# A gated hybrid layer on one core: second mixer's decay exponentials two steps sooner, the last pairs of probabilities times values at adjacent steps, output projection in 512-column products

## The chip, the cores and the metric

The kernel runs on one core of one Trainium2 chip. The metric is the device time of one execution in microseconds. A core has five engines that run side by side, each through its own instructions in order: TensorE (PE in the profile, with PEld for its weight loads), VectorE (DVE), ScalarE (ACT), GpSimd (POOL), and SyncE (SP), which here issues DMAs. They wait for each other by semaphores. The profiler records one execution; the median is over runs without the profiler's page.

## The reference, cut to what matters

One layer over 256 tokens of width 1024. A token-wise modulation (shift, scale and gate computed from a vector `c`) and an RMS norm give `h`. One wide projection of `h` yields thirteen pieces, which feed two mixers; their outputs are gated, added, projected once more and added to `x`.

```python
h = _rmsnorm(x, norm_w) * (1 + scale) + shift
(qa, ka, va, za, qm, km, vm, zm, om, ig, fg, ga, gm) = jnp.split(h @ w_in, SPLIT_IDX, axis=-1)
...
ya = merge(_moba_attention(qa, ka, heads(va, ATT_HEADS), rel_bias))
ya = (ya * jax.nn.silu(za)) @ w_att_proj
...
qk = jax.nn.silu(_causal_dwconv(jnp.concatenate([qm, km], axis=-1), conv_w, conv_b))
hm = _mlstm_chunkwise(q, k, v, ig + b_igate, fg + b_fgate)
...
ym = (merge(hm).astype(x.dtype) * jax.nn.silu(zm)) @ w_ml_proj
y = jax.nn.sigmoid(ga) * ya + jax.nn.sigmoid(gm) * ym
return x + gate * (y @ w_out)
```

The first mixer is causal attention of 8 heads of 128 over the 256 tokens, with a bias by distance. The second is a linear attention of 4 heads of 256, in which a score of a query t and a key s is multiplied by a decay exp(e_s - m_t), where e and the running maximum m come from cumulative sums of the log forget gates and the input gates.

## The kernel before, in words

**Products.** Every large product is done in three: both operands are split into a high part (rounded by a cast) and a low part (the rest), and high x high, high x low and low x high are added in PSUM. The weights come from HBM as f32 into `raw` buffers of 1 MB; ScalarE casts a piece to `wh` (line 448), and VectorE (for a few steps GpSimd) subtracts to get `wl` (line 452).

**Steps.** After a first phase (normalisation, modulation, and the projections for the attention's queries and keys) the rest is a list of chunks of 512 output columns, four steps each; a step takes two blocks of 128 rows of the contraction. In the order of the list, with the steps of each: va 0 to 11, za 12 to 19, qm 20 to 27, km 28 to 35, the attention's projection att 36 to 43, then zm, vm, om, ga, gm, the second mixer's projection ml, and out. A chunk is of one of two kinds. In "ws" chunks (za, qm, km, att, ga, gm, ml) the weights are stationary and the 256 tokens stream: 24 products of 256 columns a step (lines 1006 to 1009). In "tok" chunks the tokens are stationary and 512 weight columns stream: 12 products a step (lines 999 to 1001; 344 columns wide for va). The chunks of out have code of their own: the first half in lines 987 to 994, the second in lines 1011 to 1022.

**Order.** The program's order is written out by hand. In step g the main loop (a) splits the weights of step g + 4, with the functions of `hooks_between` put between cast and subtraction, (b) at a chunk's first step evicts the chunk before and takes an accumulator, (c) calls the step's functions in `hooks`, in the order in which `at(step, fn)` registered them, (d) issues the weight loads that have become possible (`pump`), and (e) issues the step's products. Each engine runs what falls to it in that order. `at(s, f)` puts f into step s.

**Buffers.** Accumulators of chunks ("mm") rotate through two PSUM buffers, so chunk n + 2 can start only when chunk n has been read out. Smaller products ("aux") rotate through four. There are five `wh` and five `wl` buffers.

**What the change and the steps of the prediction touch.**

- `conv` (lines 676 and 682) reads a chunk of qm or km out of PSUM: for each quarter of two blocks ScalarE does the last tap with the bias (two instructions), then VectorE the three others (six). qm's first half is read in steps 24 and 25, and the SiLU of each (line 687) follows a step later.
- The second mixer's decay is prepared by `gates_0` to `gates_7`, `gates_T` and `gates_D`. `gates_5` (step 17) writes -m to a DRAM buffer `md`, and to GE an exponential (line 565). `gates_6` reads `md` back, spread over all partitions, into `NM`. `gates_7` copies and masks NM on GpSimd. `gates_T` transposes GE on TensorE (line 587) and VectorE copies the result to `gc` (line 589). `gates_D` is eight exponentials of ScalarE on NM with gc as bias (lines 595 and 596). NM is used from the chunk zm on.
- `att_PT` transposes one head's probabilities on TensorE and copies them. `att_av` (lines 642 to 650) takes a pair of heads: four products of values and probabilities on TensorE, the multiplication by `za` on VectorE (yf), a cast on ScalarE (yah), and the low part on GpSimd (yal). yah and yal are what the att chunks stream.
- `ev_out` (lines 859 to 862) evicts a piece of the output on VectorE, adds x and stores it.

Of the kernel before, what the change touches and what calls it, by code (L numbers as in the profile page):

```python
# [17 lines left out]
KT = 8  # L18
# [48 lines left out]
def tile_hybrid(ctx: ExitStack, tc: tile.TileContext, x, c, params2, w_row, w_va, ada_mod, ada_gate,  # L67
                w_in, w_att_proj, w_ml_proj, w_out, out):
    nc = tc.nc
# [94 lines left out]
    def modulate(k, parts="ij"):  # L164
        kc = slice(k, k + 1)
        src = xnT[:, k] if k else xps[0][:, 0]
        if "i" in parts:
            nc.scalar.activation(hTh[:, k], src, AF.Identity, scale=Ab[:, kc], bias=Bb[:, kc])
        if "j" not in parts:
            return  # L170
        hf[k] = ph.tile([128, S], F32, name="hf", bufs=2)
        if k:
            nc.scalar.activation(hf[k], src, AF.Identity, scale=Ab[:, kc], bias=Bb[:, kc])
        else:
            nc.vector.tensor_scalar(hf[k], src, Ab[:, kc], Bb[:, kc], op0=OP.mult, op1=OP.add)
# [4 lines left out]
    def split_hi(k, c0, c1, copy=nc.scalar.copy):  # L180
        if k not in wsp:
            wsp[k] = (ph.tile([128, NR], F32R, name="wrh", bufs=3), ph.tile([128, NR], F32R, name="wrl", bufs=3))
        copy(wsp[k][0][:, c0:c1], wrow[k][:, c0:c1])  # L183
# [49 lines left out]
    for j in range(4):  # L233
        n, q = divmod(j, 2)
        nc.tensor.matmul(pc[:, n, q * 256:(q + 1) * 256], pick[:, j:j + 1].to_broadcast([128, 128]), cparts,
                         start=q == 0, stop=q == 1, skip_group_check=True)
# [41 lines left out]
    def some(*what):  # L278
        return lambda k: [mm_row(k, ch, (i,)) for ch, i in what]
# [23 lines left out]
    for step in P1_STEPS:  # L303
        op, k = step[0], int(step[1])
        if op == "L":
            next_loads(k)
        else:
            dict(C=modulation, H=modulate, R=rel_prep, K=keep_clock, T=x_transposes, t=x_copy, B=open_banks,
                 D=lambda k: x_transposes(k, (0,)), E=lambda k: x_transposes(k, (1,)),
                 w=lambda k: split_hi(k, 0, 512), x=lambda k: split_hi(k, 512, 1024), y=lambda k: split_hi(k, 1024, NR),  # L310
# [4 lines left out]
                 a=modulation_scale, b=modulation_shift, i=lambda k: modulate(k, "i"), j=lambda k: modulate(k, "j"),  # L315
                 P=lambda k: mm_row(k, 0), Q=lambda k: mm_row(k, 1, (0, 1)), q=lambda k: mm_row(k, 1, (2,)),
                 N=lambda k: mm_row(k, 2), M=lambda k: mm_row(k, 3),
                 n=some((2, 0), (2, 1), (3, 0), (3, 1)), m=some((2, 2), (3, 2)),
# [30 lines left out]
    def done(name, half):  # L349
        return 4 * (C[name, half] + 1)  # L350
# [83 lines left out]
    whl = {}  # L434
# [6 lines left out]
    def split(g, between=()):  # L441
        li, ks, cs = raw_of[g]
        w = rawt[li][:, ks, cs]
        n = chunks[g // 4]["n"]
        at0 = WS_AT if chunks[g // 4]["kind"] == "ws" else 0
        h = hl.tile([128, RING], F32R, name="wh", bufs=HB)[:, at0:at0 + 1024].rearrange("p (k n) -> p k n", k=2)[:, :, 0:n]
        l = hl.tile([128, RING], F32R, name="wl", bufs=HB)[:, at0:at0 + 1024].rearrange("p (k n) -> p k n", k=2)[:, :, 0:n]
        nc.scalar.copy(h, w)  # L448
        for fn, a in between:
            fn(*a)  # L450
        e = nc.gpsimd if g in pool_lo else nc.vector
        e.tensor_tensor(l, w, h.bitcast(F32), op=OP.subtract)  # L452
        whl[g] = (h, l)
# [3 lines left out]
    def at(step, fn, *a):  # L457
        hooks.setdefault(step, []).append((fn, a))
# [201 lines left out]
    def ev_za(pt, half):  # L660
        if half == 0:
            T["za"] = slot("s0", [128, AH, S], F32, "zat")
        nc.scalar.activation(T["za"][:, 4 * half:4 * half + 4], pt, AF.Silu)
# [191 lines left out]
    def ev_out(pt, c0, n, t):  # L855
        cs = slice(c0, c0 + n)
        o = hl.tile([128, n], F32, name="o", tag="scr", bufs=2)
        if c0 < 512:
            nc.vector.tensor_tensor(o, pt, T["gateb"][:, cs], op=OP.mult)
            pt = o  # L860
        nc.vector.tensor_tensor(o, pt, T["x"][:, t, cs], op=OP.add)
        nc.sync.dma_start(o2[:, t, cs], o)
# [23 lines left out]
    for h in range(AH):  # L886
# [1 line left out]
        between(A0 + h, att_qk, h)  # L888
        hooks_between.setdefault(A0 + 3 + h, []).insert(0, (att_PT, (h,)))
        at(A0 + h, att_exp, h)  # L890
    for step, fn in ((12, gates_3), (14, gates_copy), (15, gates_4), (17, gates_5), (19, gates_6), (20, gates_7),
                     (21, gates_T), (23, gates_D)):
        at(step, fn)
    for nm in ("qm", "km"):
        for hf in range(2):
# [3 lines left out]
                at(s + q + 1, conv_silu, hf, nm, q)  # L899
    for q in range(2):  # L900
        at(done("za", 0) + 2 + 2 * q, att_av, 2 * q)
        at(done("za", 1) + 2 + 2 * q, att_av, 4 + 2 * q)
    s = 4 * C["zm", 0]
    for half in range(2):
        at(s + 5 * half, ml_split, half)
# [26 lines left out]
    mmt = {}  # L932

    def pump():
        n = 0
        while n in consumed:
            n += 1
        issue(n + 6)
# [11 lines left out]
    for g in range(NG):  # L950
        ci, kp = divmod(g, 4)
        ch = chunks[ci]
        if g + A < NG:
            split(g + A, hooks_between.get(g, []))
            consumed.update(li for li in cons.get(g + A, []) if li not in gate_loads)
        if kp == 0:
            if ci > 0:
                pc = chunks[ci - 1]
                if pc["name"] in EV and ci - 1 != C["za", 0]:
                    EV[pc["name"]](mmt[ci - 1], pc["half"])  # L960
                elif pc["name"] == "out":
                    for t in range(2):
                        ev_out(mmt[ci - 1][:, t], pc["half"] * 512, 512, t)
            sh = [128, 2, 512] if ch["kind"] == "tok" else [128, 4, 256]
            if ci < NCH - 1:
                mmt[ci] = ps.tile(sh, F32, name="mm", bufs=2)
                if ch["kind"] == "tok":
                    mmt[ci] = mmt[ci][:, :, 0:ch["n"]]
        for fn, a in hooks.get(g, []):
            fn(*a)  # L970
        if g == A0 + AH - 1:
            ev_za(mmt[C["za", 0]], 0)
        if g in gate_left:
            consumed.add(gate_left[g])
        pump()
        if g == NG - 8:
            load_x()
        sh_, sl_ = (hTh, hTl) if ch["stat"] is None else (T[stat[ch["stat"]][0]], T[stat[ch["stat"]][1]])
        wh, wl = whl[g]
        if ci == NCH - 1:  # L980
            continue
        for kk in range(2):
            k = 2 * kp + kk
            first, last = k == 0, k == KT - 1
            if ch["name"] == "out":

                for i in (0, 1):
                    for t, c0 in ((0, 0), (0, 256), (1, 0), (1, 256)):
                        a = (sh_, sl_)[i][:, k, t * 128:(t + 1) * 128]
                        cs = slice(c0, c0 + 256)  # L990
                        for w in (wh, wl)[:2 - i]:
                            nc.tensor.matmul(mmt[ci][:, t, cs], a, w[:, kk, cs],  # L992
                                             start=first and i == 0 and c0 == 0 and w is wh,
                                             stop=last and i == 1 and c0 > 0, skip_group_check=True)
            elif ch["kind"] == "tok":
                for t in range(2):
                    a, b = sh_[:, k, t * 128:(t + 1) * 128], sl_[:, k, t * 128:(t + 1) * 128]
                    o = mmt[ci][:, t]
                    nc.tensor.matmul(o, a, wh[:, kk], start=first, stop=False)  # L999
                    nc.tensor.matmul(o, a, wl[:, kk], start=False, stop=False)  # L1000
                    nc.tensor.matmul(o, b, wh[:, kk], start=False, stop=last)  # L1001
            else:
                for i in range(4):
                    cs = slice(i * 128, (i + 1) * 128)
                    o = mmt[ci][:, i]
                    nc.tensor.matmul(o, wh[:, kk, cs], sh_[:, k], start=first and i % 2 == 0, stop=False,  # L1006
                                     skip_group_check=True)
                    nc.tensor.matmul(o, wh[:, kk, cs], sl_[:, k], start=False, stop=False, skip_group_check=True)  # L1008
                    nc.tensor.matmul(o, wl[:, kk, cs], sh_[:, k], start=False, stop=last and i % 2 == 1,  # L1009
                                     skip_group_check=True)  # L1010
    ci = NCH - 1
    for t, c0, n in ((0, 0, 512), (1, 0, 256), (1, 256, 256)):
        pt = ps.tile([128, n], F32, name="mm", bufs=2)
        for k in range(KT):
            a, b = T["yh"][:, k, t * 128:(t + 1) * 128], T["yl"][:, k, t * 128:(t + 1) * 128]
            for c1 in range(0, n, 256):
                wh, wl = (w[:, k % 2, c0 + c1:c0 + c1 + 256] for w in whl[4 * ci + k // 2])
                o = pt[:, c1:c1 + 256]
                nc.tensor.matmul(o, a, wh, start=k == 0 and c1 == 0, stop=False, skip_group_check=True)  # L1019
                nc.tensor.matmul(o, a, wl, start=False, stop=False, skip_group_check=True)  # L1020
                nc.tensor.matmul(o, b, wh, start=False, stop=k == KT - 1 and c1 + 256 == n, skip_group_check=True)  # L1021
        ev_out(pt, 512 + c0, n, t)


# [51 lines left out]
```

## Time and profile before

| | |
|---|---|
| median of 3 runs | 357.51 us (357.04 to 357.94) |
| the profiled execution | 357.09 us |
| its span | 355.2 us |
| its mean granted TensorE clock | 0.995 |
| HBM read, written | 76.14 MB, 1.25 MB |

How to read the profile: the page gives, for each engine, the time in which it was busy, its share of the span and its instructions; the chain that ended last (what released what, followed back from the last instruction); and groups of instructions. A timeline's row gives start and duration in us, the engine, the line of the kernel, the operation, the tile written and the tiles read, the shape, and the count of instructions merged in the row; in brackets stands the idle time before it and what ended it. A stretch's row gives its window, then for each of PE, PEld, DVE, ACT and POOL the busy time and the count, then the granted TensorE clock (1.00 is full), the DMA share and GB/s. Products on TensorE overlap in a pipeline: a row's duration is that of one product from start to end, and what a product costs in a row of them is the distance between starts.

### The profile page before, as it was taken

The page shows a single profiled execution, that of the slowest core. Times are in us where ns is not written, and L with a number is a line of the kernel's source. Part 1 is how long each engine was busy: PE and PEld are TensorE (multiplying, and loading weights), DVE is VectorE, ACT ScalarE, POOL GpSimd, SP SyncE. Part 2 cuts the span into 40 slices and gives each one's busy share as a digit, 9 for nine tenths or more (in the row PEclk, how much of TensorE's full clock was granted, in tenths as well). Part 3 has the DMA queues.
Part 4 walks back from the last instruction along what each step waited for, and adds up shares of the span by engine and source line. Part 5 has one row for each costly group of instructions (what it writes and reads, how often), then busy time and mean ns, then how long its engine had stood idle before and what let it go on. Part 6 is the DMA issues. An engine that isn't in the chain of part 4 may idle for free.

```text
span 355.2 us, 6174 instructions
## 1 busy us (share of the span) xinstructions
PE 346.5 (98%) x2432; PEld 325.6 (92%) x2432; DVE 245.9 (69%) x369; ACT 213.5 (60%) x331; POOL 90.8 (26%) x81
## 2 busy tenths in 40 slices
PE   6999999999999997999999999999999999999996
PEld 6887889999999997999998888888899999999996
DVE  6999987967975326768875593764465874569861
ACT  4868889799777376666636554545646364544410
POOL 5700004950205261554104252000011320451000
PEclk9999999999999999899999999999999999999999
DMA  8999999880741850394784837649219129191011
GB/s 304 414 416 415 415 419 405 247 316 14 275 189 60 258 218 0 127 387 137 279 317 128 346 118 238 237 158 382 53 45 375 54 99 369 68 294 62 2 61 59
DMA packets 23516, 77.79 MB, mean 219 GB/s; under 512 B 3000, under 2 KB 4928, under 8 KB 22848
## 3 DMA queue, kind: packets, MB, share of 16 engines
q1 hardware_dynamic: 23336, 76.87, 58.8%
q10 hardware_dynamic: 152, 0.53, 0.4%
q8 instruction: 19, 0.31, 0.3%
q14 instruction: 9, 0.07, 0.1%
HBM read 76.14 MB, written 1.25 MB: 218 GB/s over the span
## 4 chain that ended last, share of the span: by engine, by line
PE 93%; ACT 2%; DVE 2%; DMA 1%; issue 0%; POOL 0%; DVEq 0%; ACTq 0%; POOLq 0%
PE mm L1006 14%; PE mm L1008 14%; PE mm L1009 14%; PE pm L198 12%; PE mm L999 8%; PE mm L1000 8%; PE mm L1001 8%; PE mm L992 3%; DVE qmT L682 1%; PE xps L263 1%; DMA xt<-in_x_dram 1%; PE mm L1021 1%; PE mm L1020 1%; PE mm L1019 1%; PE aux L492 1%; PE aux L604 1%
## 5 line engine op out<-in xcount | busy, mean ns | idle before, releaser
L452 DVE TENSOR_TENSOR wl<-raw,wh 128x1024 fp32r<-128x1024 f32 (+1 forms) x92 | 117.6, 1289 | 65.7 <-ACT wh L448 65.7
L448 ACT CAST wh<-raw 128x1024 fp32r<-128x1024 f32 (+1 forms) x100 | 100.4, 1014 | 59.8 <-PE mm L1008 25.7
L1006 PE MATMUL mm<-hTh,wh 128*128 128x256 f32 x320 | 91.2, 285 | 2.3 <-DVE qmT L682 2.3
L1008 PE MATMUL mm<-hTl,wh 128*128 128x256 f32 x320 | 89.7, 280 | 0.0
L1009 PE MATMUL mm<-hTh,wl 128*128 128x256 f32 x320 | 89.6, 280 | 0.0
L1006 PEld LDWEIGHTS mm<-hTh,wh 128*128 128x128 f32 x320 | 61.2, 191 | 2.5 <-issue 2.4
L1008 PEld LDWEIGHTS mm<-hTl,wh 128*128 128x128 f32 x320 | 60.9, 190 | 0.0
L1009 PEld LDWEIGHTS mm<-hTh,wl 128*128 128x128 f32 x320 | 60.8, 190 | 0.0
L999 PE MATMUL mm<-wh,hTh 128*128 128x512 f32 (+1 forms) x144 | 53.0, 368 | 0.0
L1000 PE MATMUL mm<-wl,hTh 128*128 128x512 f32 (+1 forms) x144 | 52.6, 365 | 0.0
L1001 PE MATMUL mm<-wh,hTl 128*128 128x512 f32 (+1 forms) x144 | 52.6, 365 | 0.0
L1001 PEld LDWEIGHTS mm<-wh,hTl 128*128 128x128 f32 x144 | 27.0, 188 | 3.8
L999 PEld LDWEIGHTS mm<-wh,hTh 128*128 128x128 f32 x144 | 27.1, 188 | 3.6
L1000 PEld LDWEIGHTS mm<-wl,hTh 128*128 128x128 f32 x144 | 27.1, 188 | 3.5
L452 POOL TENSOR_TENSOR wl<-raw,wh 128x1024 fp32r<-128x1024 f32 x8 | 19.5, 2458 | 21.9 <-ACT wh L448 14.9
L183 ACT CAST wrh<-raw 128x512 fp32r<-128x512 f32 (+1 forms) x24 | 18.2, 761 | 7.5 <-DMA raw<-in_w_row_dram 7.5
L188 DVE TENSOR_TENSOR wrl<-raw,wrh 128x512 fp32r<-128x512 f32 (+1 forms) x26 | 20.5, 813 | 1.0 <-ACT wrh L183 1.0
L198 PE MATMUL pm<-wrh,hTh 128*128 128x512 f32 x64 | 19.9, 391 | 0.0
L198 PE MATMUL pm<-wrh,hTl 128*128 128x512 f32 x64 | 19.7, 389 | 0.0
L198 PE MATMUL pm<-wrl,hTh 128*128 128x512 f32 x64 | 18.7, 391 | 0.0
L682 DVE SCALAR_TENSOR_TENSOR qmT<-mm,prm,qmT 128x255 f32<-128x255 f32 (+2 forms) x24 | 9.7, 475 | 12.2 <-ACT qmT L676 12.1
L1006 PE MATMUL mm<-ymh,wh 128*128 128x256 f32 x64 | 18.0, 281 | 0.0
(218 smaller groups left out, 669.4 us busy)
## 6 DMA issues: line engine op xcount, KB each, us to landing
raw<-in_w_in_dram SPq DMA_DIRECT2D x32, 1024.0 KB, 5.0
adat<-in_ada_mod_dram SPq DMA_DIRECT2D x16, 512.0 KB, 8.8
raw<-in_w_va_dram SPq DMA_DIRECT2D x6, 688.0 KB, 8.9
raw<-in_ada_gate_dram SPq DMA_DIRECT2D x4, 1024.0 KB, 6.9
raw<-in_w_att_proj_dram SPq DMA_DIRECT2D x4, 1024.0 KB, 5.1
raw<-in_w_ml_proj_dram SPq DMA_DIRECT2D x4, 1024.0 KB, 5.9
raw<-in_w_out_dram SPq DMA_DIRECT2D x4, 1024.0 KB, 6.3
raw<-in_w_row_dram SPq DMA_DIRECT2D x15, 256.0 KB, 8.1
```

The lines of the kernel that those rows point to most:

```text
L183: copy(wsp[k][0][:, c0:c1], wrow[k][:, c0:c1])
L188: e.tensor_tensor(l[:, cs], wrow[k][:, cs], h[:, cs].bitcast(F32), op=OP.subtract)
L198: nc.tensor.matmul(pm[ch][:, t], a[:, k, t * 128:(t + 1) * 128], b[:, cs], start=k == 0 and i == 0, stop=k == KT - 1 and i == 2)
L448: nc.scalar.copy(h, w)
L452: e.tensor_tensor(l, w, h.bitcast(F32), op=OP.subtract)
L682: nc.vector.scalar_tensor_tensor(d, pt[:, i, :S - sh], col(P_CW + 16 * j + base + i), d, op0=OP.mult, op1=OP.add)
L999: nc.tensor.matmul(o, a, wh[:, kk], start=first, stop=False)
L1000: nc.tensor.matmul(o, a, wl[:, kk], start=False, stop=False)
L1001: nc.tensor.matmul(o, b, wh[:, kk], start=False, stop=last)
L1006: nc.tensor.matmul(o, wh[:, kk, cs], sh_[:, k], start=first and i % 2 == 0, stop=False, skip_group_check=True)
L1008: nc.tensor.matmul(o, wh[:, kk, cs], sl_[:, k], start=False, stop=False, skip_group_check=True)
L1009: nc.tensor.matmul(o, wl[:, kk, cs], sh_[:, k], start=False, stop=last and i % 2 == 1, skip_group_check=True)
```

## The change

Three edits, all to the order and the form of work; what is computed stays.

1. Of the second mixer's decay: the read of `md` moves from step 19 to 18, the masks from 20 to 19, the transposes of GE from 21 to 18 (behind the read, ahead of the pair of heads 0 and 1 of that step), and the eight exponentials from 23 to 21.
2. `att_av` of heads 4 and 5 moves from step 22 to 21, and that of heads 6 and 7 from step 24 to 22 (`done("za", 1)` is 20). In step 21 it stands behind the exponentials.
3. The output projection's products of 256 columns become products of 512 columns wherever the accumulator's piece is 512 wide: in the first half of the columns all, in the second half those of the first 128 tokens. The order over blocks of the contraction and over the three partial products stays, but for the two column halves of a product that are now one. The last two pieces of 256 columns stay.

```diff
@@ -888,8 +888,8 @@
-    for step, fn in ((12, gates_3), (14, gates_copy), (15, gates_4), (17, gates_5), (19, gates_6), (20, gates_7),
-                     (21, gates_T), (23, gates_D)):
+    for step, fn in ((12, gates_3), (14, gates_copy), (15, gates_4), (17, gates_5), (18, gates_6), (18, gates_T),
+                     (19, gates_7), (21, gates_D)):
         at(step, fn)
@@ -899,7 +899,7 @@
     for q in range(2):
         at(done("za", 0) + 2 + 2 * q, att_av, 2 * q)
-        at(done("za", 1) + 2 + 2 * q, att_av, 4 + 2 * q)
+        at(done("za", 1) + 1 + q, att_av, 4 + 2 * q)
@@ -985,13 +985,11 @@
                 for i in (0, 1):
-                    for t, c0 in ((0, 0), (0, 256), (1, 0), (1, 256)):
+                    for t in range(2):
                         a = (sh_, sl_)[i][:, k, t * 128:(t + 1) * 128]
-                        cs = slice(c0, c0 + 256)
                         for w in (wh, wl)[:2 - i]:
-                            nc.tensor.matmul(mmt[ci][:, t, cs], a, w[:, kk, cs],
-                                             start=first and i == 0 and c0 == 0 and w is wh,
-                                             stop=last and i == 1 and c0 > 0, skip_group_check=True)
+                            nc.tensor.matmul(mmt[ci][:, t], a, w[:, kk], start=first and i == 0 and w is wh,
+                                             stop=last and i == 1)
@@ -1013,12 +1011,10 @@
             a, b = T["yh"][:, k, t * 128:(t + 1) * 128], T["yl"][:, k, t * 128:(t + 1) * 128]
-            for c1 in range(0, n, 256):
-                wh, wl = (w[:, k % 2, c0 + c1:c0 + c1 + 256] for w in whl[4 * ci + k // 2])
-                o = pt[:, c1:c1 + 256]
-                nc.tensor.matmul(o, a, wh, start=k == 0 and c1 == 0, stop=False, skip_group_check=True)
-                nc.tensor.matmul(o, a, wl, start=False, stop=False, skip_group_check=True)
-                nc.tensor.matmul(o, b, wh, start=False, stop=k == KT - 1 and c1 + 256 == n, skip_group_check=True)
+            wh, wl = (w[:, k % 2, c0:c0 + n] for w in whl[4 * ci + k // 2])
+            nc.tensor.matmul(pt, a, wh, start=k == 0, stop=False)
+            nc.tensor.matmul(pt, a, wl, start=False, stop=False)
+            nc.tensor.matmul(pt, b, wh, start=False, stop=k == KT - 1)
         ev_out(pt, 512 + c0, n, t)
```

## The prediction

> **What bounds the kernel now.** I read the page first, then what TensorE waited for, then stretches by clock, then the timelines of the stretch that stood out.
>
> ```profile
> span 355.2 us, 6174 instructions
> PE 346.5 (98%) x2432; PEld 325.6 (92%) x2432; DVE 245.9 (69%) x369; ACT 213.5 (60%) x331; POOL 90.8 (26%) x81
> PE 93%; ACT 2%; DVE 2%; DMA 1%; issue 0%; POOL 0%; DVEq 0%; ACTq 0%; POOLq 0%
> ```
>
> TensorE is the bound, and 93% of the chain that ended last is its. A change can save only by taking products away, by making them faster, or by removing a wait of TensorE. After the start-up there is one wait (who waited for whom, TensorE's rows):
>
> ```profile
> PE mm L1006 <- DVE qmT L682: 2.3, 1, 2.3
> ```
>
> The stretches around it, with TensorE's busy time and number of products, then the other engines, the granted clock near the end of the row:
>
> ```profile
> 139.10:141.38 2.28, 0.01 (x2) 0.04 (x1) 2.28 (x7) 0.66 (x2) 0.00 (x0) 0.93 0.00 0
> 141.38:144.50 3.12, 3.12 (x15) 3.12 (x16) 0.98 (x1) 3.12 (x5) 1.53 (x1) 0.50 0.45 168
> 144.50:186.00 41.50, 41.50 (x368) 41.50 (x368) 33.19 (x55) 24.64 (x33) 13.22 (x6) 1.00 0.70 252
> 284.60:330.00 45.40, 45.40 (x388) 45.40 (x387) 31.01 (x28) 21.79 (x25) 13.08 (x5) 1.00 0.48 174
> ```
>
> The wait costs twice: behind it the granted clock is 0.50 for 3.12 us. The price, from TensorE's timeline (start, duration):
>
> ```profile
> 138.83 0.28 PE L1009 MATMUL mm<-hTh,wl 128*128 128x256 f32 x1
> 141.38 0.55 PE L1006 MATMUL mm<-hTh,wh 128*128 128x256 f32 x1 [2.27 <-DVE qmT L682]
> 144.61 0.28 PE L1006 MATMUL mm<-hTh,wh 128*128 128x256 f32 x1
> ```
>
> From 138.83 to 144.61 there are 16 starts in 5.78 us. Fast products start every 41.50/368 = 0.113 us, so 16 would take 1.81. The wait and its slow clock together cost **3.97 us**.
>
> Why it waits: step 28 (km's first) needs the "mm" buffer of qm's first half, which the two convolutions of steps 24 and 25 read. ScalarE before that:
>
> ```profile
> 124.15 1.05 ACT L448 CAST wh<-raw 128x1024 fp32r<-128x1024 f32 x1 [0.50 <-PE mm L1008]
> 125.22 1.28 ACT L595 ACT_TABLE_LOAD   x1
> 126.51 0.51 ACT L595 ACTIVATE NM<-NM,gc 128x256 f32<-128x256 f32 x1
> 129.00 0.39 ACT L596 ACTIVATE NM<-NM,gc 128x128 f32<-128x128 f32 x1
> 129.29 1.04 ACT L448 CAST wh<-raw 128x1024 fp32r<-128x1024 f32 x1
> 130.24 1.00 ACT L676 ACTIVATE qmT<-mm,prm 128x256 f32<-128x256 f32 x2
> 134.34 0.62 ACT L649 CAST yah<-yf 128x512 fp32r<-128x512 f32 x1 [3.10 <-DVE yf L648]
> 134.87 1.05 ACT L448 CAST wh<-raw 128x1024 fp32r<-128x1024 f32 x1
> 135.93 1.28 ACT L687 ACT_TABLE_LOAD   x1
> 137.76 1.01 ACT L676 ACTIVATE qmT<-mm,prm 128x256 f32<-128x256 f32 x2
> ```
>
> and VectorE:
>
> ```profile
> 131.28 2.43 DVE L682 SCALAR_TENSOR_TENSOR qmT<-mm,prm,qmT 128x255 f32<-128x255 f32 x6 [8.28 <-ACT qmT L676]
> 133.62 0.69 DVE L648 TENSOR_TENSOR yf<-aux,zat 128x512 f32<-128x512 f32 x1
> 138.80 2.43 DVE L682 SCALAR_TENSOR_TENSOR qmT<-mm,prm,qmT 128x255 f32<-128x255 f32 x6 [1.37 <-ACT qmT L676]
> ```
>
> The eight decay exponentials of step 23 and their table load hold ScalarE from 125.22 to 129.3, so the first convolution starts late. Then yah of the last pair (att_av 6, step 24) makes ScalarE wait 3.10 us for VectorE, which has the convolution in front of yf; the weight cast, the table load, SiLU and the second convolution follow. It ends at 141.23, and step 28 starts at 141.38.
>
> **The change part by part.** The bursts and the decay's other pieces:
>
> ```profile
> 105.02 0.60 PE L642 MATMUL aux<-PT,vat 128*128 128x256 f32 x2
> 116.79 0.31 PE L587 MATMUL aux<-ident,GE 36*128 36x36 f32 x2
> 119.96 0.60 PE L642 MATMUL aux<-PT,vat 128*128 128x256 f32 x2
> 121.19 0.37 PE L1006 MATMUL mm<-hTh,wh 128*128 128x256 f32 x1
> 126.73 0.59 PE L642 MATMUL aux<-PT,vat 128*128 128x256 f32 x2
> 104.55 0.42 ACT L565 ACTIVATE GE<-G 4x256 f32<-4x256 f32 x1 [0.89 <-DVE st L622]
> 119.05 0.23 DVE L589 COPY gc<-aux 128x72 f32<-128x72 f32 x1
> 113.65 2.21 POOL L581 TENSOR_SCALAR_AFFINE_SELECT NM<-NM 128x512 f32<-128x512 f32 x2
> 104.14 0.33 SPq L567 DMA_DIRECT2D md<-G  x1
> 105.42 0.38 SPq L573 DMA_DIRECT2D NM<-md  x1
> 114.79 4.75 SPq L376 DMA_DIRECT2D raw<-in_w_in_dram  x2
> ```
>
> *NM's read (19 to 18) and mask (20 to 19).* The read is issued right behind md's write already, and SyncE's next load comes at 114.79, so no load is held up. GpSimd's masks stay between the same two yal and end at 115.86. Nothing.
>
> *GE's transposes (21 to 18).* On TensorE they move ahead of att_av 0, whose first product starts at 105.02; GE is written at 104.97. From VectorE's last write to the start of step 28 passed 0.15 us, so TensorE may wait about 0.1; bounds 0 and 0.3. Joining a burst, they cost about 0.2 in place of 0.44 alone (116.79 to 117.03 plus some 0.2 of slow first products). gc's 0.23 us goes ahead of yf on VectorE, and ScalarE's yah and GpSimd's yal are that much later, with nothing of TensorE behind them.
>
> *Exponentials (23 to 21).* They pass the casts of steps 22 and 23 and the yah of two pairs. Their inputs (masks 115.86, gc by about 110) are there before ScalarE reaches them.
>
> *Pairs 4 and 6 (22 and 24 to 21 and 22).* Each burst takes 119.96 to 121.19 = 1.23 us wherever it stands. Nothing on TensorE; on VectorE, yf leaves the convolutions alone.
>
> Now step by step, with a step of 24 products = 2.72 us. TensorE leaves step 20 at 117.0 (116.79 + 0.2). Step 21: burst, products, done 120.95. Step 22: the same, 124.9. Step 23: 127.6; 24: 130.35; 25: 133.1; 26: 135.8; 27: **138.5**, where step 28 wants its buffer.
> ScalarE: cast of step 21 117.0 to 118.05, table load to 119.35, exponentials (126.51 to 129.39 = 2.88) to 122.2; yah 4, cast, yah 6 (yf at 125.7), cast: 127.3. The cast of step 24 needs step 23's end: 127.6 to 128.65; L676 twice to 129.6; VectorE's six to 132.05. The cast of step 25 130.35 to 131.4, table load to 132.7, SiLU 0.6, L676 to 134.25, VectorE's six to **136.7**. The buffer is free 1.8 us before step 28: no wait. Late next: the later halves, which go at the same pace without exponentials.
>
> These edits: -3.97 for the wait and its clock, -0.2 for the joined burst, +0.1 at the transposes.
>
> The Trainium skill, "ScalarE: Activation LUTs", section "What ACT_TABLE_LOAD costs", speaks against this: a switch of table sets would cost about 2.66 us with its drain. By it the two loads would bring the second convolution some 2.5 us later, to 139.2, and leave a wait of 0.7. The rows do not agree: the load at 125.22 took 1.28 and the next instruction starts at 126.51.
>
> *Output projection in 512 columns.* First half: 96 products of 256 become 48 of 512; second half: the first 48 become 24, the last 48 stay 256 wide. Starts of the first block, and of 512-wide ones elsewhere (30 apart):
>
> ```profile
> 329.92 0.28 PE L992 MATMUL mm<-wh,yh 128*128 128x256 f32 x1
> 340.87 0.28 PE L1019 MATMUL mm<-wh,yh 128*128 128x256 f32 x1
> 187.59 0.39 PE L1001 MATMUL mm<-wh,hTl 128*128 128x512 f32 x1
> 194.39 0.39 PE L1001 MATMUL mm<-wh,hTl 128*128 128x512 f32 x1
> ```
>
> 6.80/30 = 0.2267 for 512 columns against twice 0.113; the first block takes 10.95 now and 48 x 0.2267 = 10.88 after. TensorE is paid by columns, so halving the instructions brings at most 0.07; if the last 48 fall to the slower pace below, 0.2 is lost. I take 0. Evictions and stores stay.
>
> The Trainium skill, "TensorE: Matmul & The Clock Gate", section "Back-to-back issue gap", gives N/2.4 + 2.5 ns per product, by which 72 products fewer would save 72 x 2.5 ns = 0.18 us. Here two narrow ones take the time of a wide one, so the trace shows no such fixed part.
>
> **Sum:** -4.07. The profiled execution took 357.09 (span 355.2 and 1.9 around it), so 353.0; the median of the runs shown, 357.51, lies 0.42 higher, so **353.4**.
>
> **Rivals.**
> *Slow pace (355.6).* Products of 256 columns run at two paces at full clock: 41.50/368 = 0.113 and 45.40/388 = 0.117. A pace holds for a long stretch, and I see no other cause than how a burst of small products ends. Before, steps 25 to 43 ran fast. If the burst of step 22 leaves the slow pace until the 512-wide products at 186, 22 steps x 24 x 0.0042 = 2.2 us are lost. For it: the long slow stretch. Against: the pair bursts that stood alone, at steps 22 and 24, were left fast.
> *The late stretch turns fast (351.7).* 388 x 0.0042 = 1.6 gained, if the shift in time flips it. Against: its code is unchanged.
> *A rest of the wait (353.5 to 357).* The 1.8 us are used up on ScalarE; each further us costs one, and with the slow clock (3.12 us at half, 1.56) up to 4. Both causes are moved away, so it is small; the table-load rule belongs here.
> *The change does not do what it says (357.5).* Then exponentials and pairs were not what delayed the convolutions. Against: the rows above.
> *Slower (358.6 and more).* TensorE waits in order at GE's transposes in step 18, with att_av 0 and step 18's products queued behind. It decides once the wait exceeds 4.07 less 1.56 for a slow clock behind it, 2.5 us; a wait of 3.6 gives 358.6. GE's exponential would have to end at 108.6 instead of 104.97, and nothing ahead of it on ScalarE or VectorE is moved.
>
> **How the numbers follow.** Forecast 0.52, slow pace 0.26, late fast 0.07, rest of a wait 0.07, no effect 0.05, slower 0.03. The range 351.5 to 356.0 takes in the forecast, both paces and most of the rest (bounds: transposes 0.3, last products 0.2, the 0.4 between runs); it leaves out about 0.1. A measurement can tell 0.3%, 1.07 us, from no change: faster needs under 356.4, which all cases but the last two give, save part of the rest of a wait. Faster 0.90, same 0.06, slower 0.04.
>
> **What would show it.** Right: no wait of TensorE on qmT, granted clock 1.00 from 139 to 145, exponentials near 119 to 122, L682's second six ending about 1.8 us before step 28; the first output block still about 10.9 us. Wrong: a wait at step 28 or at the transposes; exponentials waiting for NM; steps 22 to 43 at 0.117; an output block that shrinks by more than 0.1 us, which would mean instructions are paid too.

## The result and the profile after

The changed kernel took 351.71 us in the median of 6 runs (351.45 to 352.68) against 357.41 (357.04 to 357.94): ratio 0.984, 95% interval 0.983 to 0.986. The prediction was 353.4, range 351.5 to 356.0. The profiled execution took 351.62, with a span of 349.8, 5.4 us less than before.

The page after, the span and the engines' row:

```profile
span 349.8 us, 6030 instructions
PE 344.9 (99%) x2360; PEld 320.0 (91%) x2360; DVE 246.5 (70%) x369; ACT 213.4 (61%) x331; POOL 91.6 (26%) x81
```

All that TensorE waited for:

```profile
PE warm L227 <- POOL ident masks.py:199: 1.4, 1, 1.4
PE xps L263 <- ACT diag L246: 0.2, 1, 0.2
```

Both lie in the start-up; the wait on the convolution is gone. The stretches that answer to those of before (window, PE, PEld, DVE, ACT, POOL, clock, DMA share, GB/s):

```profile
138.60:141.40 2.80, 2.80 (x27) 2.80 (x26) 0.37 (x2) 2.58 (x4) 2.01 (x1) 1.00 0.56 187
141.40:182.00 40.60, 40.60 (x361) 40.60 (x359) 33.31 (x55) 24.38 (x32) 12.74 (x6) 1.00 0.71 260
280.50:324.10 43.60, 43.60 (x387) 43.60 (x386) 29.98 (x28) 21.63 (x25) 13.78 (x5) 1.00 0.50 182
```

The clock stays at 1.00 where it was 0.50. The last row is the surprise: steps 76 to 91 ran 388 products in 45.40 us before and run 387 in 43.60 now, 0.113 us each and not 0.117, though nothing was changed there.

Setting the start of each step in one trace against its start in the other shows where the 5.43 us up to the last product come from:

| stretch | gained, us |
|---|---|
| start-up to step 17 | 0.15 |
| steps 18 to 27 | 0.20 |
| the wait at step 28 and the slow clock | 3.97 |
| steps 29 to 67 | 0.00 |
| steps 68 to 75 | -0.21 |
| steps 76 to 91 | 1.69 |
| output projection | -0.37 |

ScalarE, then VectorE, in the steps 21 to 25 of the changed kernel:

```profile
118.09 1.28 ACT L595 ACT_TABLE_LOAD   x1
121.88 0.39 ACT L596 ACTIVATE NM<-NM,gc 128x128 f32<-128x128 f32 x1
122.17 0.60 ACT L649 CAST yah<-yf 128x512 fp32r<-128x512 f32 x1
130.56 1.05 ACT L448 CAST wh<-raw 128x1024 fp32r<-128x1024 f32 x1 [0.75 <-ACT qmT L676]
132.35 1.28 ACT L687 ACT_TABLE_LOAD   x1 [0.73 <-DVE qmT L682]
134.18 1.00 ACT L676 ACTIVATE qmT<-mm,prm 128x256 f32<-128x256 f32 x2
...
129.84 2.43 DVE L682 SCALAR_TENSOR_TENSOR qmT<-mm,prm,qmT 128x255 f32<-128x255 f32 x6 [4.00 <-ACT qmT L676]
135.22 2.43 DVE L682 SCALAR_TENSOR_TENSOR qmT<-mm,prm,qmT 128x255 f32<-128x255 f32 x6 [1.54 <-ACT qmT L676]
```

The exponentials end at 122.27. The second convolution ends at 137.65 and step 28 starts at 138.59: 0.94 us to spare. The output part, first product of each block and last product (the blocks are the first half of the columns, the wide piece of the second, the two narrow pieces):

```profile
324.12 0.39 PE L991 MATMUL mm<-wh,yh 128*128 128x512 f32 x1
335.31 0.39 PE L1015 MATMUL mm<-wh,yh 128*128 128x512 f32 x1
340.88 0.28 PE L1015 MATMUL mm<-wh,yh 128*128 128x256 f32 x1
346.21 0.28 PE L1017 MATMUL mm<-wh,yl 128*128 128x256 f32 x1
```

72 wide products in 16.76 us are 0.2328 each, not the 0.2267 of zm, vm and om.

### The profile page after: what moved, and what is told of

It is laid out like the page before. It is cut to its first block, busy times and chain, and to the rows that moved or that the text cites. A ratio compares the mean times of both kernels' runs of the same rounds, so it can differ in the third digit from the quotient of the medians.

```text
span 349.8 us, 6030 instructions
## 1 busy us (share of the span) xinstructions
PE 344.9 (99%) x2360; PEld 320.0 (91%) x2360; DVE 246.5 (70%) x369; ACT 213.4 (61%) x331; POOL 91.6 (26%) x81
## 4 chain that ended last, share of the span: by engine, by line
PE 98%; ACT 1%; POOL 0%; DVE 0%; issue 0%; POOLq 0%
PE mm L1007 15%; PE mm L1006 15%; PE mm L1004 15%; PE pm L198 13%; PE mm L997 8%; PE mm L998 8%; PE mm L999 8%; PE mm L991 3%; PE xps L263 1%; PE mm L1017 1%; PE mm L1015 1%; PE aux L642 1%; PE mm L1016 1%; PE aux L492 1%; PE aux L604 1%; PE aux L762 1%
## 5 line engine op out<-in xcount | busy, mean ns | idle before, releaser
L1004 PE MATMUL mm<-hTh,wh 128*128 128x256 f32 x320 | 90.0, 281 | 0.0
L1006 PE MATMUL mm<-hTl,wh 128*128 128x256 f32 x320 | 88.7, 277 | 0.0
L1007 PE MATMUL mm<-hTh,wl 128*128 128x256 f32 x320 | 88.7, 277 | 0.0
L1004 PEld LDWEIGHTS mm<-hTh,wh 128*128 128x128 f32 x320 | 60.3, 188 | 0.0
L1006 PEld LDWEIGHTS mm<-hTl,wh 128*128 128x128 f32 x320 | 60.2, 188 | 0.0
L1007 PEld LDWEIGHTS mm<-hTh,wl 128*128 128x128 f32 x320 | 60.1, 188 | 0.0
L1007 PE MATMUL mm<-yah,wl 128*128 128x256 f32 x64 | 17.7, 276 | 0.0
L1004 PE MATMUL mm<-yah,wh 128*128 128x256 f32 x64 | 17.7, 276 | 0.0
```

## The experiments

Three questions were open. Which edit cleared the wait? Why did steps 76 to 91 become fast? Why is the wide output projection slower?

### One edit at a time

`exp_only` is the kernel before with the first edit alone:

```diff
-    ... (19, gates_6), (20, gates_7),
-                     (21, gates_T), (23, gates_D)):
+    ... (18, gates_6), (18, gates_T),
+                     (19, gates_7), (21, gates_D)):
```

> The kernel before with the decay's pieces moved alone (the pair of heads 6 and 7 stays in step 24, the output projection in 256 columns). Theory (both edits of the order are needed to clear the wait, each takes away most of it): ScalarE's casts and the first convolution start on time, but yah of the last pair still waits for VectorE's convolution in front of yf; the second convolution ends about 139.0, and step 28, ready at 138.6, waits 0.3 to 0.6 us, too short to slow the clock: 353.5 to 354.2 with the paces of before. Rival (the exponentials alone made the wait): no wait, the transposes' 0.4 paid, 353.0 to 353.5. Rival (the last pair made the wait): 357.

Measured: 352.83 us, ratio 0.987 (0.984 to 0.991). ScalarE, VectorE and TensorE around step 28:

```profile
132.90 0.62 ACT L649 CAST yah<-yf 128x512 fp32r<-128x512 f32 x1 [3.10 <-DVE yf L648]
...
137.36 2.43 DVE L682 SCALAR_TENSOR_TENSOR qmT<-mm,prm,qmT 128x255 f32<-128x255 f32 x6 [1.37 <-ACT qmT L676]
...
139.81 0.28 PE L1009 MATMUL mm<-hTh,wl 128*128 128x256 f32 x1
139.93 0.36 PE L1006 MATMUL mm<-hTh,wh 128*128 128x256 f32 x1
```

yah still waits 3.10 us for yf, and yet step 28 follows its predecessor after 0.12 us. The convolution ends at 139.79, just in time. The theory that both edits were needed fell: with the decay's pieces moved alone, TensorE no longer waits. Steps 76 to 91 were fast here as well. Its time is still 1.3 us above that of `order_only` below, but this is mostly not the pairs: of the 1.64 us between the two profiled executions 1.33 arise in the start-up, ahead of step 0, whose first product starts at 54.9 to 56.2 us in the thirteen traces.

`pairs_only` has the second edit alone:

```diff
-        at(done("za", 1) + 2 + 2 * q, att_av, 4 + 2 * q)
+        at(done("za", 1) + 1 + q, att_av, 4 + 2 * q)
```

> The kernel before with the last two pairs at steps 21 and 22 alone. Theory: the exponentials in step 23 still hold ScalarE, the first convolution is as late as before (its first instruction near 131), but the second follows without the 3.1 us wait for yf; it ends about 139.6, step 28 is ready near 138.6 and waits about 1 us: 354 to 354.8 without a slow clock, 356 with one. Rival (the exponentials alone made the wait): a wait over 2 us stays, 357. Rival (the last pair alone made it): no wait, 353.4.

Measured: 355.43 us, ratio 0.996 (0.994 to 0.999). What TensorE waited for, and the stretches behind:

```profile
PE mm L1006 <- DVE qmT L682: 1.5, 1, 1.5
...
141.17:144.20 3.03, 3.03 (x26) 3.03 (x27) 0.99 (x1) 3.03 (x5) 1.44 (x1) 1.00 0.53 172
144.20:186.00 41.80, 41.80 (x357) 41.80 (x356) 33.68 (x55) 24.49 (x33) 13.33 (x6) 1.00 0.69 252
```

A wait of 1.5 us stays, where the theory said about 1, and the clock stays at 1.00 behind it. But steps 29 to 43 run at 41.80/357 = 0.117: the slow pace that the prediction feared, in another kernel. This profiled execution, 357.05 us, is one of the slowest of the ten; four took 354.5 to 354.7, within the 354 to 354.8 expected, so the slow pace may not come in every execution; no trace shows this. So the pairs alone are worth 0.8 us of wait, and about 1.7 of clock in an execution where the clock would have fallen; with the exponentials moved as well they are the 0.94 us to spare.

`order_only` has both and leaves the output projection as it was, `out_only` is the third edit alone (the diff of the output projection as above).

> Both edits of the order, the output projection as before. Theory (the output projection in 512 columns costs about 0.4 us, since its products start every 0.233 us and not every 0.2267): the output part takes 21.7 us from its first product to its last, not 22.1; the time is that of the changed kernel less 0.3 to 0.4 if steps 76 to 91 run at the fast pace (351.3), and about 1.7 more at the slow one (353.0). Rival (the narrow form fell to the slow pace without the change of width, and the loss is the pace's): the output part takes 22 us or more.

> The kernel before with the output projection in 512-column products alone. Theory: the wait at step 28 and its slow clock stay (4.0 us); the output part takes 22.1 us and not 21.7, so 357.8 with the paces of before. Rival (fewer instructions pay): 357.2 or less with the paces of before. If steps 76 to 91 run at the fast pace, either is 1.7 less; their pace is read from the trace.

Measured: `order_only` 351.51 us, ratio 0.984 (0.981 to 0.988); `out_only` 357.95, ratio 1.001 (0.998 to 1.003). The times cannot tell either from its neighbour. The traces can; first and last product of the output part of `order_only`:

```profile
324.02 0.28 PE L992 MATMUL mm<-wh,yh 128*128 128x256 f32 x1
...
345.66 0.28 PE L1021 MATMUL mm<-wh,yl 128*128 128x256 f32 x1
```

21.65 us narrow, 22.09 wide (324.12 to 346.21), and 22.10 in `out_only`. The wide form costs 0.44 us.

### The pace of steps 76 to 91

In `exp_only` and `order_only` these steps were fast, in `pairs_only` and `out_only` slow. In TensorE's order the two groups differ in two things: whether TensorE waits at step 28, and where GE's transposes stand. Three kernels tell these apart. `before_again` is the kernel before unchanged. `transposes_only` moves the transposes (with the read of `md` and the masks) but leaves the exponentials, and so the wait:

```diff
-    ... (19, gates_6), (20, gates_7),
-                     (21, gates_T), (23, gates_D)):
+    ... (18, gates_6), (18, gates_T),
+                     (19, gates_7), (23, gates_D)):
```

`late4` is `order_only` with a wait made by hand: in `conv`, two instructions of step 25 are done four times:

```diff
-        for i in ii:
+        for i in ii * (4 if (nm, half, q) == ("qm", 0, 1) else 1):
             nc.scalar.activation(T[nm][:, 4 * half + i], pt[:, i], AF.Identity, ...
```

> The kernel before, once more. Theory (the order of slow and fast paces is set by the program): the paces of all steps are those of the first trace, steps 76 to 91 slow, the wait 2.3 us with the slow clock: 357.0 to 357.5. Rival (each execution falls into its own order of paces): steps 76 to 91 can be fast, 355.7.

> The kernel before with the read, the masks and GE's transposes moved as in the change, the exponentials left in step 23 and the pairs where they were. Theory: the wait at step 28 and the slow clock stay as before (2.3 us, 4.0 with the clock), since only the exponentials hold ScalarE; 357.2 with the paces of before. On the paces: if the place of the transposes in TensorE's order sets steps 76 to 91, they are fast here and the time is 355.6; if the wait at step 28 does, they are slow.

> Both edits of the order, the output projection as before, and the two scale instructions in front of the second convolution of qm's first half done four times (the same value each time), 2.7 to 2.9 us more of ScalarE in step 25. In the changed kernel that convolution ended 0.94 us before step 28 was ready, so a wait of 1.8 to 1.9 us should stand at step 28. Theory (a wait there costs itself, and brings the slow clock only from about 2 us on): clock 1.00, 353.3 plus what the paces do; with the slow clock 355. On the paces: if a wait at step 28 is what makes steps 76 to 91 slow, they are slow here (1.7 more); if the place of the transposes in TensorE's order is, they are fast.

Measured, one execution each: 355.77, 357.23 and 355.40 us. The rows of `before_again` (the wait and what follows it), of `transposes_only` (behind the wait, and steps 76 to 91) and of `late4` (the wait, behind it, and steps 76 to 91):

```profile
139.20:141.49 2.29, 0.02 (x2) 0.03 (x1) 2.29 (x7) 0.67 (x2) 0.00 (x0) 1.00 0.00 0
141.49:144.50 3.01, 3.01 (x26) 3.01 (x27) 0.98 (x1) 3.01 (x5) 1.42 (x1) 1.00 0.53 170
```

```profile
141.27:144.40 3.13, 3.13 (x20) 3.13 (x21) 0.98 (x1) 3.13 (x5) 1.53 (x1) 0.70 0.45 168
...
286.50:330.00 43.50, 43.50 (x386) 43.50 (x385) 29.86 (x27) 21.57 (x25) 13.47 (x5) 1.00 0.50 182
```

```profile
139.20:141.07 1.87, 0.10 (x2) 0.03 (x1) 1.87 (x6) 0.25 (x2) 0.00 (x0) 1.00 0.00 0
141.07:144.00 2.93, 2.93 (x25) 2.93 (x26) 0.98 (x1) 2.93 (x5) 1.34 (x1) 1.00 0.54 175
...
284.80:328.30 43.50, 43.50 (x386) 43.50 (x385) 29.80 (x27) 21.56 (x25) 13.88 (x5) 1.00 0.50 182
```

Of the 1.87 us of `late4`'s first row TensorE is idle for 1.77. With the transposes moved, steps 76 to 91 are fast (43.50/386 = 0.113) with a wait in front as without. In `before_again` they were slow again. That it is the wait is refuted.

`before_again` shows something else: the same wait, and no slow clock. Its 355.77 is 1.3 us under the first profiled execution. It is the time that the rival expected, but from the clock and not from steps 76 to 91. Of the 19 executions of the kernel before that were timed beside the first four experiments, ten have a mean granted clock of 0.994 or 0.995, as the three traces with the half clock have, and nine 0.998 to 1.00; so the half clock comes in about half of them. Four of the nine took 355.65 to 355.77; three others took 357.28 to 357.40, of which there is no trace.

Where the half clock starts gives a hint of why it does not always come. In `transposes_only` TensorE first runs at full clock for 1.2 us behind the wait:

```profile
141.27:142.50 1.23, 1.23 (x11) 1.23 (x12) 0.98 (x1) 1.23 (x2) 0.00 (x0) 1.00 0.16 60
142.55:145.90 3.35, 3.35 (x18) 3.35 (x18) 1.22 (x4) 2.48 (x5) 3.04 (x2) 0.50 0.36 132
146.00:148.00 2.00, 2.00 (x19) 2.00 (x18) 2.00 (x4) 1.37 (x3) 1.60 (x1) 1.00 0.00 0
```

In all three traces with it (the first of the kernel before, `out_only`, `transposes_only`) the half clock lasts 3.41 us and starts 136.53 us, forty times 3.41, after the trace's clock record begins (at 4.53, 5.35 and 6.00 us). In the 3.41 us ahead of it TensorE was idle for 1.96, 2.26 and 2.15 us. Where the wait brought no half clock, the period in which most of it falls, counted in the same way, has 1.94 (`before_again`), 1.46 (`pairs_only`) and 1.08 us (`late4`). At the programs' ends, where the products stop, it is the same: in the thirteen traces the clock falls 16 times, each time at the end of such a period with 1.96 us or more idle, and never behind one with 1.94 or less. So the same wait costs the half clock or not by how it falls on these periods. This was read out of the traces afterwards; no run moved a wait across a period's edge, and 1.94 against 1.96 is a thin margin.

The pace of steps 29 to 43 behind a wait is not settled: slow in `pairs_only`, `late4` and `transposes_only`, fast in `before_again`, `out_only` and the first trace of the kernel before. It is why `transposes_only` missed its 355.6 with fast steps 76 to 91: steps 28 to 43 took 46.81 us, and 45.06 in the first trace of the kernel before. It is also most of why `late4` lies above its 353.3.

Then the reverse: `trans21_exp22` moves the exponentials one step, so that the wait goes, and leaves the transposes alone in step 21. `trans19` is `order_only` with the transposes in step 19.

```diff
# trans21_exp22, against the kernel before
-    ... (19, gates_6), (20, gates_7), (21, gates_T), (23, gates_D)):
+    ... (18, gates_6), (19, gates_7), (21, gates_T), (22, gates_D)):
# trans19, against order_only
-    ... (18, gates_6), (18, gates_T), (19, gates_7), (21, gates_D)):
+    ... (18, gates_6), (19, gates_T), (19, gates_7), (21, gates_D)):
```

> The kernel before with the read, the masks and the exponentials one step sooner each (18, 19, 22), the transposes left alone in step 21, the pairs in 22 and 24. Theory (the exponentials make the wait, the place of the transposes sets the late pace, and these are two separate gains): no wait at step 28, clock 1.00, and steps 76 to 91 slow: 353.2 to 353.8. Rival (the late pace goes with the wait at step 28): no wait and steps 76 to 91 fast: 351.6 to 352.1.

> Both edits of the order with the transposes in step 19 and not 18, the output projection in 256 columns. Theory (the 0.2 us gap in front of the transposes in step 18 is the wait for GE's exponential; a step later it is there): 0.1 to 0.2 us less than with step 18, 351.2 to 351.4 if the late pace stays fast. Which pace follows is not known beforehand: if it is enough that the transposes share a burst, steps 76 to 91 are fast; if it hangs on the very step, they may be slow, 353.

> The changed kernel once more. Theory: the paces of its first trace, step by step, no wait at step 28, the output part 22.1 us; 351.5 to 351.9. Rival (each execution falls into its own paces): steps 76 to 91 slow in this trace, 353.3.

Measured: 353.16 us (ratio 0.987, 0.982 to 0.992), 351.38 (0.981, 0.977 to 0.985) and 351.75 (0.982, 0.978 to 0.987). In `trans21_exp22`, around step 28 and in steps 76 to 91:

```profile
138.00:142.00 4.00, 4.00 (x37) 3.97 (x36) 2.00 (x4) 3.04 (x5) 1.39 (x1) 1.00 0.37 130
280.80:326.00 45.20, 45.20 (x387) 45.20 (x386) 31.72 (x28) 21.78 (x25) 13.84 (x5) 1.00 0.46 175
```

No wait, and the slow pace: two separate gains, as the theory said. One step sooner for the exponentials is enough. The read and the masks moved here too, so of what `transposes_only` moved the transposes are left. `after_again` repeated the paces of the changed kernel's first trace step by step, and so did `trans19` from step 22 on.

Over all traces: where the transposes share a burst (steps 18 or 19; eight traces of seven programs) steps 76 to 91 are fast, where they stand alone (step 21; five traces of four programs) slow. All traces take the same time for each of steps 44 to 70; fast and slow ones part at step 71, 50 steps after the transposes. Behind the burst there, the second product starts 0.201 us after the first and the rest of the step is slow in the kernel before; in the changed kernel it is 0.207 us, and the rest is fast. In steps 72 to 74 it is the other way round, and the balance is the 0.21 us lost in steps 68 to 75. What the last burst leaves, ahead of step 76, holds for 16 steps. How the order in step 18 reaches that far was not found.

The second expectation of `trans19`, 0.1 to 0.2 us less at the transposes, failed. TensorE in the changed kernel's step 18, then in `trans19`'s step 19:

```profile
104.76 0.27 PE L631 MATMUL aux<-ident,P 128*128 128x128 f32 x1
104.96 0.31 PE L587 MATMUL aux<-ident,GE 36*128 36x36 f32 x2
```

```profile
109.23 0.27 PE L631 MATMUL aux<-ident,P 128*128 128x128 f32 x1
109.44 0.31 PE L587 MATMUL aux<-ident,GE 36*128 36x36 f32 x2
```

The gap in front is 0.20 us in both, though in `trans19` GE has long been written. It is not the wait for the exponential; it goes with the product itself, the only one here whose weights have 36 rows. No run varied the rows; two products with 128 rows and 36 columns (line 523) start 0.11 us after their predecessors.

### Why the wide form is slow

`out_off0` is the changed kernel with yh and yl, the stationary operands of the output projection, at the start of their slots, 64 and 192 bytes lower:

```diff
-                T[nm] = t[:, at0:].rearrange("p (k s) -> p k s", k=KT)
+                T[nm] = t[:, 0:KT * S].rearrange("p (k s) -> p k s", k=KT)
```

> The changed kernel with yh and yl, the output projection's stationary operands, placed 64 and 192 bytes lower in the same slots. Theory (the irregular starts of the 512-wide products come from where the stationary operand lies against the moving one): another mean distance than 0.233 us for these 72 products, 0.227 if it is settled as in zm, vm and om; the output part then takes 21.6 to 21.8 us. Rival (they come from the order of the products or the accumulators): 0.233 and 22.1 us as before.

Measured, one execution: 351.72 us. The first product of each block and the last:

```profile
324.36 0.40 PE L991 MATMUL mm<-wh,yh 128*128 128x512 f32 x1
335.27 0.39 PE L1015 MATMUL mm<-wh,yh 128*128 128x512 f32 x1
340.71 0.28 PE L1015 MATMUL mm<-wh,yh 128*128 128x256 f32 x1
346.34 0.28 PE L1017 MATMUL mm<-wh,yl 128*128 128x256 f32 x1
```

The 72 wide products now take 16.35 us, 0.2271 each; the 48 narrow ones take 5.63 between first and last, 0.120 each, where they took 5.33. Where the operands lie sets the distance of starts here, and the offsets of the kernel before suit the narrow form only; which of the two offsets does it was not tried. The expected total (21.6 to 21.8) was missed, 21.98, since the narrow rest was not thought of.

Best is the change without its third edit: `order_only` 351.51 and `trans19` 351.38 against 351.71 and 351.75 for the changed kernel. The intervals overlap; that they are faster rests on the traces, not on the times: from the first product of step 0 to the last product `order_only` takes 290.81 us, `trans19` 290.91 and the changed kernel 291.25; the output part makes 0.44 us of it.

## Why the prediction was right, and where it was not

- **The wait and its slow clock, -3.97:** right, 3.97 in the traces. The mechanism named, exponentials ahead of the first convolution, is shown by `exp_only` and `trans21_exp22`, which clear the wait without moving the pairs. The other half of it, yah's wait for yf, made 0.8 of the 2.27 us (`pairs_only`) and did not need to go. And 3.97, of which 1.70 is the clock, is the price in an execution in which the clock falls; `before_again` paid the wait alone. Against the executions of before at 355.7, the change gains 4.0 us and not 5.7.
- **1.8 us to spare at step 28:** 0.94. In the schedule the table load followed the cast at 131.4; it waited for the first convolution until 132.35. The two loads took 1.28 us each and the next instruction followed at once, so the 2.66 us of the Trainium skill ("ScalarE: Activation LUTs", section "What ACT_TABLE_LOAD costs") did not show here.
- **Transposes, -0.2 for the joined burst and +0.1 for a wait:** wrong in both. In the burst they cost TensorE 0.43 us, as alone, and the gap was no wait for GE. Steps 18 to 27 gained 0.20 by other paces, 0.09 in step 18 and 0.11 in step 24, where the pair no longer stands. That the two terms add up to about the 0.09 us that `transposes_only` gains in these steps is luck.
- **Output projection, 0 with bounds of 0.07 gained and 0.2 lost:** mis-sized: 0.37 lost against the trace of before, 0.44 against `order_only`. The failed step is that a wide product would start every 0.2267 us as in zm, vm and om; with these stationary operands it is 0.2328, and the first block took 11.19 us and not about 10.9. The 2.5 ns per product of the Trainium skill ("TensorE: Matmul & The Clock Gate", section "Back-to-back issue gap"), which that section gives for isolated products, did not show either: at the better offset a wide product costs what two fast narrow ones do.
- **Nothing at 76 to 91, with a chance of 0.07 that they turn fast:** the rival came in, with 1.69 us. It is the largest part of the 1.7 us between forecast and result, but that the two agree is luck: 0.21 in steps 68 to 75 and 0.37 in the output part were lost, while the start-up gave 0.15, steps 18 to 27 0.1 more than forecast, and the 0.42 put on top of the profile for the median was 0.09 after. The result lies only 0.21 above the low end of the range. The reason against the rival, that the code there is unchanged, did not hold: in all thirteen traces the pace goes with an order 50 steps earlier. The slow pace of steps 22 to 43, given 0.26, stayed out of the changed kernel and came in from step 28 on in `pairs_only`.

## What to carry to other kernels

When the bound engine waits once, follow the waiting buffer to the engine whose queue made it late, and move what stands ahead there; here eight exponentials two steps sooner were worth 2.3 us of wait, and 4 with the half clock behind it; one step would have done, and moving the pairs as well gave slack. Before joining narrow products into wide ones, look at the distance of their starts and not at their count: paid by columns, joining brings nothing, and operand offsets chosen for one width can be wrong for the other. A gain of a percent may be an accident of pace: compare the distance of starts in stretches that the change does not touch before crediting it to an edit.

## What the runs showed that was not expected

- Products of 256 columns hold one of two paces, 0.113 or 0.117 us, over as much as 45 us, at full clock. A burst of small products can change it. The two programs that were traced twice show the same pace in the same step both times.
- A wait of 2.26 or 2.27 us brought 3.41 us of half clock in three traces and not in a fourth; waits of 1.46 and 1.77 did not, in one trace each. The half clock can start 1.2 us after the products do.
- A product with weights of 36 rows starts 0.20 to 0.21 us after its predecessor, in all three places where it stood.
- 64 and 192 bytes of offset of the stationary operands change wide products from 0.2328 to 0.2271 us and narrow ones from 0.113 to 0.120.
